# A state space scan in two passes of two channel groups, on pairs of real and imaginary part

## The chip, the cores and the metric

The kernel runs on one core of one Trainium2 chip. The metric is device time in microseconds (us) of one execution; the numbers are medians of three runs. TensorE multiplies matrices, VectorE, ScalarE and GpSimd compute elementwise, and SyncE, ScalarE and GpSimd also issue DMAs, each on a queue of its own. [...]

## What is computed

The program is two transformer blocks on 256 latent and 256 context tokens of width 1024: attention, then a state space layer (S5), then a second block. The change is in S5. Each of its 128 groups of 16 channels has 64 complex states in each of two directions; a state goes on by x(t+1) = a x(t) + B u(t). It runs over the context first and goes on over the latents; only the latents' outputs are wanted.

```python
def _s5_direction(u_ctx, u_lat, lam, dt, bmat, cmat):
    ...
    def run(u, h0):
        ...
        h_fin, ys = lax.scan(step, h0, chunks)
        return h_fin, ys.swapaxes(0, 1).reshape(bsz, n, S5_GROUPS * S5_GROUP)

    h0 = jnp.zeros((u_lat.shape[0], S5_GROUPS, S5_STATE), jnp.complex64)
    h_ctx, y_ctx = run(u_ctx, h0)
    _, y_lat = run(u_lat, h_ctx)
    return y_ctx, y_lat
```

The outputs go through gelu and two large products (`glu`, `w_out`).

## The kernel before, in words

All products are of float32 values as a high and a low part. A weight piece [128, 1024] (`weight`) arrives by a DMA on SyncE's queue, ScalarE casts its high part (L97) and VectorE subtracts the low one (L98); there are two buffers for the parts, so a cast waits until TensorE is done with the piece before the last one. Three matmuls make one product (L119 to L121).

S5 (`s5_layer`) works in blocks of 8 tokens, 32 of the context and 32 of the latents, and on four channel groups b = 0 to 3 of 32 pairs (direction, state pair) by 128 partitions. For each b there are

- four linears `u(b, j)`: 48 matmuls each. `s5_store_u` copies the result on ScalarE (two instructions, tile `s_ut`) and stores it to DRAM from ScalarE's queue; `s5_load_u` brings it back in another layout (tile `s_U`) from GpSimd's queue. It is a transposition by way of DRAM.
- `s5_blocks`: four steps a of 64 small matmuls (tile `vps`), which give what each block adds to the states. Each needs one operator of 1 MB (`d_rt`). ScalarE copies the result to `s_V`.
- `s5_scan` on VectorE: 16 steps, each of two products, a sum over both parts, and a difference and a sum over one part each (L493 to L497). Five levels of a tree over the 32 blocks of the context; then seven steps in which four runs of eight latent blocks go on side by side; then three that carry from run to run. A last pair of copies (L517) turns the second direction.
- `s5_out`: four steps of 16 matmuls on `s_U` (`within`) and 64 on the states (`across`). Each step's `across` needs one operator of 1 MB (`d_o`), each two `within` another (`d_t`). Two copies (`s_ysb`) and eight transposes (`ytps`) end it.

Between them stand eleven `gate` linears (24 matmuls each). TensorE and VectorE keep the order that the code is written in (`self.ordered`). `run(scan, us)` writes as many steps of the scan as go with that much of TensorE's time, so the numbers in the `yield`s and in `run` place each weight's L98 among the scan's instructions. The operators go through a ring of five buffers (`operator`); after the first four, GpSimd's queue issues them, in order with the loads of `s_U`. Scan b stands beside the linears of b + 1 and the outputs of b - 1.

## Time and profile before

| | us |
|---|---|
| median of three runs | 1501.27 |
| lowest and highest run | 1500.88, 1508.71 |
| span of the profiled execution, first to last instruction | 1494.4 |
| median less that span | 6.9 |
| TensorE busy in the span | 1379.3 (92%) |
| VectorE busy in the span | 1152.3 (77%) |
| S5's scans, first to last of VectorE's instructions | 673.9 to 871.2 |

The page has one execution; times within it are counted from its first instruction. It gives the span and no time of its own for that execution, so the 6.9 us stand for what lies around. The share of TensorE over the whole span hides that S5 is another stage than the rest: there the table by stretches has to be read.

### The profile page before, as it was taken

The numbers are of one execution on the slowest core, as the hardware profiler recorded it, in microseconds if no ns is written. First come the engines' busy times: TensorE is split into PE (matmuls) and PEld (weight loads), VectorE is DVE, ScalarE is ACT, GpSimd is POOL, SyncE is SP. The second block draws the span as 40 slices with busy tenths as digits, with TensorE's granted clock in tenths as the row PEclk, the third lists the DMA queues.
The fourth block names the chain that finished last, engine by engine and source line by source line (L and its number), as shares of the span: only waits on it lengthen the run. The fifth ranks groups of instructions, "written<-read, shape, count | busy, mean of one in ns | idle before, by whom it ended". The sixth has DMA issues, their size and how long they took to land.

```text
span 1494.4 us, 30436 instructions
## 1 busy us (share of the span) xinstructions
PE 1379.3 (92%) x12192; PEld 1201.1 (80%) x12192; DVE 1152.3 (77%) x2122; ACT 712.5 (48%) x1307; POOL 100.5 (7%) x221
## 2 busy tenths in 40 slices
PE   5889979999999998898877779999998999999997
PEld 4657656667777778798866669999998999999996
DVE  7989886787768779839988966755568876788887
ACT  4434435655555544622244244544447556565554
POOL 0012211110011011001111000000000000000000
PEclk9989988999999999999988989999999999999999
DMA  9459984454435444578787676555555544445552
GB/s 359 160 170 319 297 247 127 141 156 143 140 120 156 149 131 139 174 223 282 276 294 281 246 266 212 194 194 198 184 183 164 171 169 141 158 171 192 187 184 99
DMA packets 140622, 291.35 MB, mean 195 GB/s; under 512 B 30480, under 2 KB 70080, under 8 KB 135104
## 3 DMA queue, kind: packets, MB, share of 16 engines
q1 hardware_dynamic: 108592, 232.01, 45.5%
q0 software_dynamic: 11360, 49.34, 10.4%
q10 hardware_dynamic: 20528, 8.06, 2.0%
q8 instruction: 95, 1.56, 0.4%
q14 instruction: 47, 0.39, 0.1%
HBM read 234.83 MB, written 54.53 MB: 194 GB/s over the span
## 4 chain that ended last, share of the span: by engine, by line
PE 69%; DVE 15%; issue 7%; DMA 6%; ACT 2%; POOL 0%; SPq 0%; DVEq 0%; ACTq 0%; POOLq 0%
PE lin L119 14%; PE lin L120 14%; PE lin L121 13%; PE modps L591 3%; DVE s_t L493 3%; DVE wl L98 2%; DMA sp_x<-in_s_bcw_dram 2%; PE slat L119 2%; DMA d_o<-sp_o 1%; PE sctx L119 1%; PE dn L121 1%; PE dn L119 1%; PE dn L120 1%; DVE s_V L495 1%; DVE sp_t L37 1%
## 5 line engine op out<-in xcount | busy, mean ns | idle before, releaser
L97 ACT CAST wh<-wr 128x1024 fp32r<-128x1024 f32 x268 | 280.5, 1048 | 407.2 <-PE lin L120 250.0
L98 DVE TENSOR_TENSOR wl<-wr,wh 128x1024 fp32r<-128x1024 f32 x268 | 327.5, 1223 | 148.2 <-ACT wh L97 147.7
L119 PE MATMUL lin<-prH,wh 128*128 128x256 f32 x512 | 145.3, 284 | 0.0
L119 PE MATMUL lin<-yaH,wh 128*128 128x256 f32 x512 | 144.8, 283 | 0.0
L120 PE MATMUL lin<-yaL,wh 128*128 128x256 f32 x512 | 144.6, 282 | 0.0
L121 PE MATMUL lin<-prH,wl 128*128 128x256 f32 x512 | 143.7, 281 | 1.0 <-DVE wl L98 1.0
L121 PE MATMUL lin<-yaH,wl 128*128 128x256 f32 x512 | 144.1, 281 | 0.0
L120 PE MATMUL lin<-prL,wh 128*128 128x256 f32 x512 | 143.8, 281 | 0.2 <-DVE prL L109 0.2
L120 PEld LDWEIGHTS lin<-prL,wh 128*128 128x128 f32 x512 | 96.7, 189 | 1.7 <-DVE prL L109 0.6
L119 PEld LDWEIGHTS lin<-yaH,wh 128*128 128x128 f32 x512 | 97.5, 190 | 0.0
L119 PEld LDWEIGHTS lin<-prH,wh 128*128 128x128 f32 x512 | 96.7, 189 | 1.0
L121 PEld LDWEIGHTS lin<-yaH,wl 128*128 128x128 f32 x512 | 97.4, 190 | 0.0
L120 PEld LDWEIGHTS lin<-yaL,wh 128*128 128x128 f32 x512 | 97.3, 190 | 0.0
L121 PEld LDWEIGHTS lin<-prH,wl 128*128 128x128 f32 x512 | 96.3, 188 | 1.2 <-DVE wl L98 1.2
L493 DVE TENSOR_TENSOR s_t<-s_V,s_tab 128x256 f32<-128x256 f32 (+2 forms) x120 | 73.2, 652 | 15.7 <-ACT s_V L475 14.5
L121 PE MATMUL u<-h,wl 128*128 128x256 f32 x224 | 66.0, 295 | 9.3 <-DVE wl L98 9.3
L427 POOL DMA_DIRECT2D d_t<-sp_g x128 | 66.8, 529 | 56.9 <-DVE sp_g L37 52.6
L121 PE MATMUL lin<-h,wl 128*128 128x256 f32 x128 | 42.4, 331 | 29.7 <-DVE wl L98 29.7
L119 PE MATMUL u<-h,wh 128*128 128x256 f32 x224 | 66.1, 295 | 0.0
L120 PE MATMUL u<-h,wh 128*128 128x256 f32 x224 | 65.6, 293 | 0.5 <-issue 0.5
L119 PE MATMUL lin<-hH,wh 128*128 128x512 f32 x144 | 60.6, 421 | 0.7 <-ACT hH L103 0.7
L37 DVE TENSOR_TENSOR sp_t<-s_pb,sp_x 128x1024 f32<-128x1024 f32 x64 | 60.0, 952 | 0.6
(481 smaller groups left out, 3871.8 us busy)
## 6 DMA issues: line engine op xcount, KB each, us to landing
wr<-in_glu_dram SPq DMA_DIRECT2D x64, 512.0 KB, 3.3
wr<-in_w_up_dram SPq DMA_DIRECT2D x44, 512.0 KB, 4.2
wr<-in_w_in_dram SPq DMA_DIRECT2D x32, 512.0 KB, 4.8
mraw<-in_w_mod_dram SPq DMA_DIRECT2D x64, 256.0 KB, 3.1
d_rt<-sp_rt SPq DMA_DIRECT2D x64, 256.0 KB, 4.0
d_o<-sp_o SPq DMA_DIRECT2D x32, 512.0 KB, 4.8
wr<-in_s_in_dram SPq DMA_DIRECT2D x32, 512.0 KB, 4.5
s_op<-d_o POOLq DMA_DIRECT2D x16, 1024.0 KB, 7.9
```

What stands on the lines that cost most here:

```text
L37: return lambda *a, **k: self.net.in_order(f(*a, **k))
L97: self.in_order(nc.scalar.copy(hi, raw))
L98: self.in_order(nc.vector.tensor_tensor(lo, raw, hi.bitcast(F32), SUB))
L119: self.in_order(t.matmul(out, a[0], b[0], start=start, stop=False))
L120: self.in_order(t.matmul(out, a[0], b[1], start=False, stop=False))
L121: self.in_order(t.matmul(out, a[1], b[0], start=False, stop=stop))
L427: nc.gpsimd.dma_start(self.d_t[k].rearrange("s i j e c -> i s j e c")[:, :, j, e], a)
L493: go(v.tensor_tensor(t[:, x], src.to_broadcast([128, 2, 32, n]), a[x].unsqueeze(1).to_broadcast([128, 2, 32, n]), MUL))
L495: go(v.tensor_tensor(dst, dst, t[:, 0], ADD))
L591: self.in_order(nc.tensor.matmul(p[32 * j:32 * j + 32, :w], self.cs[:, kc, :], raw[:, jj * w:jj * w + w], start=(kc == 0), stop=(kc == 7), ...
```

## The change

The four channel groups are scanned two at a time, so there are two scans instead of four, with rows of 64 pairs. Real and imaginary part lie side by side. A step is two products and two sums, all over both parts; the second product reads the pairs swapped and multiplies by (-imaginary, imaginary). The context's blocks lie in a tile of their own (`s_C`) with a tree of four levels and one step into the last block; then the latents' 32 blocks go one by one in 31 steps (`s_V`, `at`). Both directions read their own block, so there is no reversal at the end. The multipliers are the powers 1, 2, 4, 8 and 16 alone.

`U` is one tile with context and latents apart, so `d_u` is written in runs of 32 floats (128 bytes) instead of 64, and each load is two DMAs. In S5 `s_ut` has one buffer instead of two, and the operators' ring four instead of five. The order is written anew: blocks 0, four linears, blocks 1; scan 0 beside six linears and blocks 2 and 3; scan 1 beside the outputs 0 and 1 and all eleven gates; then the outputs 2 and 3.

```diff
     def s5_scratch(self):
...
-        self.d_u = d.tile([4, 4, 8, 128, 64], F32, name="d_u")
+        self.d_u = d.tile([4, 4, 8, 2, 128, 32], F32, name="d_u")
...
-    def s5_store_u(self, b, j, ps, tp):
+    def s5_store_u(self, b, j, ps, tp, bufs=2):
...
-        nc.scalar.dma_start(self.d_u[b, j].rearrange("s p k -> p s k")[:, ::-1], ut.rearrange("p s g k -> p s (g k)"))
+        nc.scalar.dma_start(self.d_u[b, j].rearrange("s g p k -> p (s g) k"), ut.rearrange("p s g k -> p (s g) k"))
...
-        t = self.ops.tile([128, 2048], F32, name="s5_op", bufs=5)
+        t = self.ops.tile([128, 2048], F32, name="s5_op", bufs=4)
...
+        def step(a, src, swapped, t, base, dst):
+
+            for x, y, z in ((src, a[0], base), (swapped, a[1], dst)):
+                go(v.tensor_tensor(t, x, y.to_broadcast(t.shape), MUL))
+                go(v.tensor_tensor(dst, z, t, ADD))
+        for l in range(4):
...
+                i, o = slice(c + h - 1, e, m), slice(c + m - 1, e, m)
+                n, x = (e - c) // m, Cf[:, :, o]
+                step(a, Cf[:, :, i], Cf[:, :, i, ::-1], T[:, :, 0:n], x, x)
...
+        step(one(4), x, x[:, :, :, ::-1], Tv, base, at((0, 31)))
+        for k in range(31):
+            c, o = (k, 31 - k), at((k + 1, 30 - k))
+            step(one(0), at(c), at(c, 1), Tv, o, o)
...
     def s5_layer(self, h1):
...
-                self.s5_store_u(b, j, self.u(b, j, h1), tp)
+                self.s5_store_u(b, j, self.u(b, j, h1), tp, 1)
...
+            for a in range(4):
+                st[0][2](0, a, ahead[a])
+            for b, j in ((1, 2), (1, 3), (2, 0), (2, 1)):
+                u(b, j)
+            blocks(1)
+            scan += [self.s5_scan(0, st[0], tp), 0.0]
+            for b, j in ((2, 2), (2, 3), (3, 0), (3, 1), (3, 2), (3, 3)):
+                linear(b, j)
+            st[1] = self.s5_blocks(tp)
+            blocks(2)
+            blocks(3)
+            run(scan, 1000.0)
+            scan += [self.s5_scan(1, st[1], tp), 0.0]
...
+            for b in range(2):
+                within, across, close = out(b, st[0][1])
+                for a in range(4):
+                    within(a)
+                    across(a)
+                    run(scan, 2.3)
+                    if a % 2 == 1:
                         gate(1)
...
```

How the change stands in the engines' orders, at three places. ScalarE where S5 begins, around the first blocks' copies (`s_ut` is the copy and store of a linear, `vps` the blocks' result), before:

```order
L97 CAST wh<-wr 128x1024
L438 COPY s_ut<-u 128x8x32 x2
L439 DMA d_u<-s_ut 128x8x64
L97 CAST wh<-wr 128x1024
L438 COPY s_ut<-u 128x8x32 x2
L475 COPY s_V<-vps 128x2x256
L439 DMA d_u<-s_ut 128x8x64
L475 COPY s_V<-vps 128x2x256 x7
```

and now:

```order
L97 CAST wh<-wr 128x1024
L435 COPY s_ut<-u 128x8x32 x2
L436 DMA d_u<-s_ut 128x16x32
L97 CAST wh<-wr 128x1024
L435 COPY s_ut<-u 128x8x32 x2
L436 DMA d_u<-s_ut 128x16x32
L474 COPY s_C<-vps 128x2x128
L475 COPY s_V<-vps 128x2x4x31
```

The second copy into `s_ut` now has the same buffer as the first, and the first blocks' copies, two for each bank of `vps`, stand behind it; the store's runs went from 64 floats to 32.

VectorE at the scan's way from the context's tree into the latents (`s_t` is the product, `s_tab`, `s_a`, `s_tr` and `s_ti` are multipliers), before:

```order
L493 TENSOR_TENSOR s_t<-s_V,s_a_7182 128x64 x2
L495 TENSOR_TENSOR s_V<-s_V,s_t 128x64
L496 TENSOR_TENSOR s_V<-s_V,s_t 128x32
L497 TENSOR_TENSOR s_V<-s_V,s_t 128x32
L493 TENSOR_TENSOR s_t<-s_V,s_tab 128x64x4 x2
L495 TENSOR_TENSOR s_V<-s_V,s_t 128x64x4
L496 TENSOR_TENSOR s_V<-s_V,s_t 128x32x4
L497 TENSOR_TENSOR s_V<-s_V,s_t 128x32x4
L98 TENSOR_TENSOR wl<-wr,wh 128x1024
```

and now, at the same place of scan 0:

```order
L497 TENSOR_TENSOR s_t<-s_C,s_tr 128x64x2
L498 TENSOR_TENSOR s_V<-s_C,s_t 128x2x32x2
L497 TENSOR_TENSOR s_t<-s_C,s_ti 128x64x2
L498 TENSOR_TENSOR s_V<-s_V,s_t 128x2x32x2
L98 TENSOR_TENSOR wl<-wr,wh 128x1024
L497 TENSOR_TENSOR s_t<-s_V,s_tr 128x64x2
L498 TENSOR_TENSOR s_V<-s_V,s_t 128x2x32x2
```

Four instructions of 128 elements, each reading what the one ahead of it wrote, take the place of five; this L98 is the last one in scan 0, and 31 such steps follow it.

TensorE at the end of S5 (`yps` from `s_U` is `within`, from `s_V` it is `across`; `lin<-yaH` is the first product of `glu`), before:

```order
L536 MATMUL yps<-s_op,s_U 32x128 x8
L549 MATMUL yps<-s_op,s_V 32x128 x32
L560 MATMUL ytps<-ident,s_ysb 128x128 x8
L536 MATMUL yps<-s_op,s_U 32x128 x32
L549 MATMUL yps<-s_op,s_V 32x128 x128
L560 MATMUL ytps<-ident,s_ysb 128x128 x8
L119 MATMUL lin<-yaH,wh 128x256
```

and now:

```order
L540 MATMUL yps<-s_op,s_U 32x128 x32
L553 MATMUL yps<-s_op,s_V 32x128 x128
L564 MATMUL ytps<-ident,s_ysb 128x128 x8
L540 MATMUL yps<-s_op,s_U 32x128 x8
L553 MATMUL yps<-s_op,s_V 32x128 x32
L564 MATMUL ytps<-ident,s_ysb 128x128 x8
L119 MATMUL lin<-yaH,wh 128x256
```

Before, the four `across` of one group stand behind the last scan; now those of group 2 do, and all of group 3's output (four such pairs of `within` and `across`; one is shown).

## Rows read from the trace of the kernel before

**Rows 1.** Stretches of S5: us, PE, PEld, DVE, ACT, POOL busy, clock, DMA, GB/s

```profile
660.40:673.20 12.80, 9.95 (x259) 9.42 (x257) 9.91 (x20) 5.69 (x10) 0.00 (x0) 0.87 0.83 282
673.20:721.00 47.80, 42.54 (x523) 41.41 (x523) 46.29 (x89) 14.56 (x26) 8.96 (x16) 0.96 0.80 268
721.00:771.00 50.00, 39.92 (x750) 37.21 (x750) 43.56 (x86) 15.61 (x30) 6.75 (x12) 0.86 0.82 298
771.00:821.00 50.00, 38.51 (x735) 35.15 (x732) 43.61 (x86) 18.44 (x35) 6.74 (x12) 0.90 0.77 284
821.00:871.00 50.00, 34.65 (x508) 31.07 (x510) 47.99 (x90) 12.09 (x19) 4.11 (x7) 0.90 0.67 249
```

**Rows 2.** The same for the scans' instructions alone, four scans together (tile s_V)

```profile
673.80:871.20 197.40, 14.26 (x768) 10.78 (x768) 158.34 (x328) 13.73 (x25) 0.90 0.77 275
```

**Rows 3.** Waits: who waited for whom, us in total, times, longest

```profile
PE lin L121 <- DVE wl L98: 26.6, 10, 6.1
POOL s_U L446 <- DMA d_u<-s_ut: 65.1, 10, 19.8
DVE s_t L493 <- ACT s_V L475: 14.5, 3, 6.3
```

**Rows 4.** TensorE's price of four linears, blocks of one group, one output step

```profile
637.40:660.40 23.00, 23.00 (x193) 22.93 (x192) 4.58 (x8) 5.91 (x13) 0.72 (x2) 1.00 0.65 191
763.40:771.10 7.70, 7.70 (x258) 7.63 (x257) 2.09 (x4) 6.36 (x10) 1.79 (x3) 1.00 0.61 231
866.60:868.30 1.70, 1.70 (x81) 1.26 (x80) 1.21 (x3) 1.10 (x2) 0.54 (x1) 1.00 0.83 308
```

**Rows 5.** VectorE in time, multipliers: floats alone, in twos, in fours, 32 bytes apart

```profile
658.97 0.41 DVE L334 TENSOR_TENSOR s_tab<-s_t 128x128 f32<-128x128 f32 x1
659.41 0.41 DVE L335 TENSOR_TENSOR s_t<-s_tab 128x128 f32<-128x128 f32 x1
661.43 0.43 DVE L334 TENSOR_TENSOR s_tab<-s_t 128x256 f32<-128x256 f32 x1
664.47 0.69 DVE L334 TENSOR_TENSOR s_tab<-s_t 128x512 f32<-128x512 f32 x1
```

**Rows 6.** VectorE in time: small steps of the first scan's tree

```profile
688.74 0.39 DVE L495 TENSOR_TENSOR s_V<-s_V,s_t 128x128 f32<-128x128 f32 x1
689.16 0.27 DVE L496 TENSOR_TENSOR s_V<-s_V,s_t 128x64 f32<-128x64 f32 x1
```

**Rows 7.** VectorE's groups by line and shape, 671 to 871 us: busy, mean ns

```profile
L98 DVE TENSOR_TENSOR wl<-wr,wh 128x1024 fp32r<-128x1024 f32 x22 | 26.7, 1215 | 0.8 <-ACT wh L97 0.8
L517 DVE COPY s_V<-s_V 128x496 f32<-128x496 f32 x8 | 3.0, 412 | 0.0
```

**Rows 8.** A linear's store, all stores' landing, U's loads' landing; packets by queue

```profile
L439 ACTq DMA_DIRECT2D d_u<-s_ut x1: 366/366/366, 659.8 to 659.8; - x1
DMA to landing us min/median/max: 2.8/5.6/16.0
DMA to landing us min/median/max: 2.5/3.8/7.8
q0 software_dynamic: 278, 2.02, 69.4%
q10 hardware_dynamic: 2079, 0.52, 30.1%
```

**Rows 9.** End of S5: operator's load, its landing, TensorE, the chain's last load

```profile
867.61 0.54 POOL L451 DMA_DIRECT2D s_op<-d_o  x1 [8.51 <-PE yps L536]
DMA to landing us min/median/max: 6.1/6.1/6.1
880.26 1.96 PE L549 MATMUL yps<-s_op,s_V 64*32 64x128 f32 x64 [1.36 <-DMA s_op<-d_o]
885.06 0.56 PE L119 MATMUL lin<-yaH,wh 128*128 128x256 f32 x1
872.08 8.14 DMA s_op<-d_o
```

More of the change, by code (lines that the diff above doesn't have):

```diff
@@ L475, in step @@
[L475 to L502 removed]
+                                p[64 * e:64 * e + 64, c:c + 64], rt[:, d, j, r, 64 * e:64 * e + 64],
@@ L503, in s5_scan @@
             h, m = 1 << l, 2 << l
[L504 removed]
+            a = self.tr[:, g, l].unsqueeze(2).unsqueeze(3), self.ti[:, g, l].unsqueeze(2)
+            for c in ((0, 16) if l == 0 else (0,)):
                 e = c + 16 if l == 0 else 32
[L506 to L511 removed]
@@ L1115, in s5_layer @@
             self.ordered = (mybir.EngineType.PE, mybir.EngineType.DVE)
-            st, prev = self.s5_blocks(0, tp, ahead), None
-            for a in range(4):
-                st[2](a)
-            todo = iter([(b, j) for b in range(1, 4) for j in range(4)][2:])
+            st = [self.s5_blocks(tp), None]
+            scan = []
             ya = []
@@ L1130, in low @@
                                                           ya[0][:, j:j + 2].bitcast(F32), SUB))
-            for b, (nu, early, late) in enumerate(((5, 0, 1), (3, 0, 1), (2, 1, 1), (0, 12 - NG, 0))):
-                scan = [self.s5_scan(b, st, tp), 0.0]
-                cur = st
-                if prev:
-                    within, across, close = out(b - 1, prev)
-                if b == 3:
-                    ya.append(self.big.tile([128, 16, 256], F32R, tag="s16", name="yaH", bufs=3))
-                    high(0)
-                    high(1)
-                for a in range(max(nu, 4 if prev else 0)):
-                    if a < nu:
-                        u(*next(todo))
-                        run(scan, 4.0)
-                    for _ in range((early + 3 - a) // 4):
-                        gate(1)
-                        run(scan, 2.6)
-                    if prev and a < 4:
-                        within(a)
-                        across(a)
-                        run(scan, 2.7)
-                if prev:
-                    close()
-                if b < 3:
-                    st = self.s5_blocks(b + 1, tp)
-                    for a in range(4):
-                        if a < late:
-                            gate(1)
-                            run(scan, 1.5)
-                        st[2](a)
-                        run(scan, 2.0)
-                else:
-                    high(2)
-                    within, across, close = out(3, cur)
-                    for a in range(4):
-                        within(a)
-                run(scan, 1000.0)
-                prev = cur
@@ new lines, in s5_layer @@
+            st[1] = self.s5_blocks(tp)
[3 more added lines that the diff above has]
+            scan += [self.s5_scan(1, st[1], tp), 0.0]
+            ya.append(self.big.tile([128, 16, 256], F32R, tag="s16", name="yaH", bufs=3))
+            left = 16 - NG
+            for b in range(2):
+                within, across, close = out(b, st[0][1])
+                for a in range(4):
+                    within(a)
+                    across(a)
+                    run(scan, 2.3)
+                    if a % 2 == 1:
+                        gate(1)
+                        left -= 1
+                        run(scan, 1.6)
+                close()
+                high(b)
@@ L1169, in s5_layer @@
+            for _ in range(left):
+                gate(1)
+                run(scan, 1.6)
+            within, across, close = out(2, st[1][1])
+            for a in range(4):
+                within(a)
+            run(scan, 1000.0)
             ya.append(self.big.tile([128, 16, 256], F32R, tag="s16", name="yaL", bufs=3))
@@ L1171, in s5_layer @@
                 across(a)
-                if a < 3:
+                if a < 2:
                     low(a)
+            close()
+            high(2)
+            within, across, close = out(3, st[1][1])
+            for a in range(4):
+                within(a)
+                across(a)
+            low(2)
             close()
```

132 lines of the change are left out of this document (61 added, 71 removed).

## The prediction

> **What bounds the kernel now.** I read the table by stretches first, since the change touches S5 alone and the orders of the engines ahead of it and behind it stay as they are. From 673 to 871 us VectorE is busy 43.6 to 48.0 us of every 50 [rows 1], TensorE 34.7 to 42.5, and less from stretch to stretch. The scans hold VectorE for 158.3 of 197.4 us [rows 2], 22 weights' subtractions for 26.7 [rows 7], and 14.5 go to three hand-overs, in which the next scan waits for ScalarE's copy of its blocks [rows 3]; together 199.5, the stretch but for some overlap. So VectorE sets the pace. TensorE's waits are its consequence: 26.6 us in the gates' linears for a subtraction that stands behind scan steps [rows 3]. DMA is not far behind, busy 0.67 to 0.82 [rows 1].
>
> What TensorE must do from 660.4 us to the first product of `glu` at 885.1 [rows 9] follows from three prices [rows 4]: four linears 23.0, so 5.8 each and 2.9 for a gate of half the matmuls; the blocks of a group 7.7; an output step 1.7. Ten linears, eleven gates, four groups' blocks, 16 output steps and some 4 for transposes make 58 + 32 + 31 + 27 + 4 = 152 us, in 224.7. That difference of 73 us is the most that there is to gain.
>
> **A scan step after the change.** Multipliers lying 32 bytes apart cost 0.41 us for 128 floats and 0.43 for 256 in twos [rows 5]: a float's neighbour is free. Floats alone cost 0.27 for 64 and 0.39 for 128 [rows 6]. The new step in the latents has 64 pairs, so 0.27 to 0.28 for an instruction. One that needs the one ahead of it starts 0.03 after its end (688.74 and 0.39, next at 689.16) [rows 6], and one that only overwrites what that one reads does as well (658.97 and 0.41, next at 659.41) [rows 5]. All four instructions hang together in this way: 4 x 0.305 = 1.22 us. In the tree a step of 1024 floats takes 4 x 1.25 = 5.0 (1.22 for 1024 [rows 7]), three times; 512 floats 4 x 0.72 = 2.9; 256 floats 4 x 0.46 = 1.8. With the step into the last block and 31 in the latents a scan is 15 + 2.9 + 1.8 + 32 x 1.22 = 58.7 us, two are 117.4, against 158.3 busy now. The hand-overs of 14.5 go as well, since the second scan's blocks are ready when it begins. The multipliers themselves (20 small instructions for 24) lie ahead of the first blocks' end and cost nothing either way.
>
> **What the change puts in series.** The saving of 55 us on VectorE is not the gain, because three stretches now have no scan beside them or wait for something else. I follow the path on the clock of before, from 660.4.
>
> 1. Ahead of scan 0. TensorE does blocks 0 (12.8 with their waits [rows 1]), four linears (23.2) and blocks 1 (7.7), and ScalarE copies the last bank (0.8): 704.9 at the earliest, where the first scan now starts at 673.8 [rows 2]. But the four linears (1,0) to (1,3) go through one buffer `s_ut`: each copy (0.65 for two) waits until the store before it has landed, and blocks 1 need the last one. Stores take 2.8 to 16.0 us to land, median 5.6 [rows 8], the long ones while operators load. Their runs are half as long and twice as many. The first of the four is stored at 659.8 now [rows 8]; I set it 2 us later, since the stores ahead of it have the short runs too. At 5 each the chain is hidden; at 14 it is 661.8 + 4 x 14.65 = 720.4. I take 9, because two of the four meet four operators in flight: 661.8 + 4 x 9.65 = 700.4, then the loads of `U` (two issues of 0.54 [rows 9], 3.8 to land [rows 8]) 705.3, blocks 1 713.0, copy 713.8. ScalarE's casts and the copies of blocks 0 stand behind the waiting copies; this delays blocks 0 by some 4 us, which is inside the same chain. Scan 0 starts at **714** (705 to 734).
>    Whether 9 or 14 is right hangs on how engines share their time: in a stretch with two operators and two stores in flight, 2079 store packets passed beside 278 of the operators, 7.5 to one [rows 8]. If a queue gives a fixed number of packets per turn, twice the packets take twice the turns; if a turn is one partition's packets (8 now, 16 then), the turns stay as many. [...] No run here shows which.
> 2. Scan 0. 58.7 and five subtractions at 1.13, and 0.6 for casts that come late: 65 us, to **779**. TensorE has six linears and two groups' blocks beside it, 50 us, with some 10 of waiting for operators: hidden, then idle until 779.
> 3. Scan 1. 58.7 and 13 subtractions, 73.4. Here the cover turns: a subtraction waits for its cast, the cast for the gate two before it, and the first four gates stand between the output steps of groups 0 and 1, which need 12 operators of 1 MB through a ring of four. Two loads behind the first of three took 6.5 us (first landed at 867.6 + 6.1, last at 872.08 + 8.14 [rows 9]), so 3.3 each and some 40 in all, of which four are in or under way when scan 1 begins. By this the fourth gate is done 36 us into scan 1, where VectorE asks for what depends on it at 33; its cast then makes VectorE wait some 5 us, and the cast for the seventh, which stands behind the sixth gate's silu on ScalarE, as much again. I take 10 (0 to 20). Scan 1 ends at **862**, where the last now ends at 871.2.
> 4. The tail. Now one group's `across` is left, three loads late, and `glu` starts 13.9 us after the scan (885.1 - 871.2). After the change the ring holds group 2's four operators when scan 1 ends, so all six of group 3 load from then on: 1.1 for the first `across`, 6.1 to the first landing, five more at 3.0 (less traffic beside them than the 3.3 above; bounds 2.7 and 3.5), 1.1 for the last `across` and 2.9 from there to `glu` (880.26 + 1.96, then 885.06 [rows 9]): 26.1 us. `glu` starts at **888**.
>
> That is 3 us after the 885.1 of now. The profiled span of 1494.4 becomes 1497.4; the runs' median lies 6.9 above the span, and I carry that over: 1501.3 + 3 = **1504 us**. So the saving on VectorE is spent on 40 us that pass before the first scan, on the waits in scan 1 and on a tail that is 12 us longer.
>
> **Rivals.**
>
> - *The buffers don't bind* (faster). The stores land in about 5, so scan 0 starts at 705; the gates keep ahead of VectorE, no wait in scan 1; the tail's loads come at 2.7. 705 + 65 + 73.4 + 24.6 = 868: 17 us gained, **1484**. For it speaks that half of the stores land within 5.6 us [rows 8]; against it the maximum of 16.0 there, and 65.1 us in which GpSimd waited for such stores [rows 3]. Half of it gives 1492. Chance of over 0.5% faster: 0.25.
> - *Twice the packets take twice the turns* (slower). With a fixed number of packets per turn a store beside operators lands in 14 instead of 9, scan 0 starts at 734, and the time is **1524**; from 11 each it is past 0.5%. For it speaks the 7.5 to one [rows 8], which is near the 8 runs that a partition has now; that same number speaks against it, if the turn goes by partitions. Chance 0.14.
> - *The swapped operand is slow* (slower). Read in falling order, a pair may cost as two single floats, 0.39 instead of 0.28 for 64 pairs and about twice for the tree: 64 x 0.12 + 2 x (3 x 0.9 + 0.7) = 14 us, **1518**; it decides from 0.06 a small instruction. Against it: the copies of 496 floats in falling order take 0.41 [rows 7], faster than any product of that size. Chance 0.10.
> - Scan 1 and the tail both at their upper ends (20 and 28.5): +16, **1517**. Chance 0.08.
>
> **How the numbers follow.** A measurement of this kernel tells about 0.5%, 7.5 us, from no change. The forecast, within it (1494 to 1509), has 0.43; the faster rival 0.25; the three slower ones 0.32. The predicted time is the forecast's, 1504. The range of 8 in 10 reaches to 1487 (nearly the whole of the faster rival) and to 1521 (the slow operand and the tail in it, the packets' end out); the forecast's own range is 1494 to 1509.
>
> **What would show it.** VectorE's small products at 0.28 and a step's pitch of 1.22 show the price; the swapped product beside the plain one shows the third rival. The first product on `s_C` at 714 and a row of ScalarE waiting for d_u<-s_ut show step 1; at 705 without that row, the first rival. A scan 1 of 83 us with VectorE waiting for ScalarE's casts shows step 3, of 74 not. In the tail the `yps` matmuls should wait for s_op loads, 26 us from the last scan instruction to `lin<-yaH`. I am wrong if `glu` starts ahead of 877 or after 893.

## The result and the profile after

The changed kernel takes **1524.2 us** (median of 4 runs, 1523.5 to 1525.4) where the kernel before takes 1501.1: a ratio of 1.0153, with a 95% interval of 1.0125 to 1.0180. The forecast was 1504, with a range of 1487 to 1521. So it is slower, by 23 us, and lies 3 us beyond the upper end of the range.

The executions wander by 5 to 9 us ahead of the layer, where the programs are the same. I therefore measure from a mark, the first product of the linear (0,2), which lies at 637.34 us in the profile of before and at 642.45 in that of the changed kernel (636 to 645 in the other runs). `glu` starts 247.7 us behind the mark before the change (885.06 [rows 9]) and 269.6 behind it after. Before, 36.5 of these pass until the first scan starts, 197.4 in the scans and 13.9 behind them; after, 83.8, 159.9 and 25.9. So the scans give back 37.5 us, and the stretches ahead of them and behind them take 59.3 more. These are the rows of TensorE in time in the changed kernel (start, duration, engine, line, operation; in brackets the idle time ahead and what ended it):

```profile
642.45 0.28 PE L119 MATMUL u<-h,wh 128*128 128x256 f32 x1
666.51 0.34 PE L469 MATMUL vps<-s_U,s_op 128*64 128x64 f32 x4 [0.86 <-DMA s_U<-d_u]
...
886.22 6.34 PE L553 MATMUL yps<-s_op,s_V 64*32 64x128 f32 x256 [22.26 <-DVE s_V L498]
...
898.08 1.81 PE L553 MATMUL yps<-s_op,s_V 64*32 64x128 f32 x64 [2.69 <-DMA s_op<-d_o]
...
905.53 1.96 PE L553 MATMUL yps<-s_op,s_V 64*32 64x128 f32 x64 [1.66 <-DMA s_op<-d_o]
...
912.05 0.36 PE L119 MATMUL lin<-yaH,wh 128*128 128x256 f32 x1
```

The stretches of the layer after the change, cut at the scans (us, busy time of PE, PEld, DVE, ACT, POOL, granted clock, DMA share, GB/s), which answer to [rows 1, 2]:

```profile
673.00:700.00 27.00, 25.41 (x372) 25.03 (x370) 2.45 (x2) 8.02 (x20) 3.44 (x6) 0.94 0.86 308
700.00:726.00 26.00, 17.43 (x315) 16.89 (x314) 1.23 (x1) 9.04 (x23) 6.36 (x11) 0.80 0.67 173
726.00:793.00 67.00, 53.34 (x816) 51.59 (x815) 61.88 (x153) 21.13 (x52) 12.60 (x22) 0.95 0.81 263
793.00:886.00 93.00, 58.16 (x968) 52.75 (x968) 70.81 (x162) 28.43 (x50) 8.22 (x14) 0.79 0.66 248
886.00:912.00 26.00, 18.42 (x591) 14.79 (x592) 3.87 (x7) 6.68 (x16) 3.57 (x6) 0.76 0.67 251
```

VectorE, busy through 673 to 871 before, now does next to nothing for 53 us (2.45 and 1.23 busy), works through scan 0, idles a quarter of scan 1 and has nothing to do in the tail. Its groups by line and shape from 726 to 886 us (busy, mean ns, idle time before and who ended it), which answer to [rows 6, 7]:

```profile
L498 DVE TENSOR_TENSOR s_V<-s_V,s_t 128x128 f32<-128x128 f32 x126 | 37.0, 294 | 4.3
L98 DVE TENSOR_TENSOR wl<-wr,wh 128x1024 fp32r<-128x1024 f32 x18 | 22.0, 1221 | 17.5 <-ACT wh L97 17.3 <-issue 0.2
L497 DVE TENSOR_TENSOR s_t<-s_V,s_ti 128x128 f32<-128x128 f32 x62 | 18.2, 293 | 2.1
L497 DVE TENSOR_TENSOR s_t<-s_V,s_tr 128x128 f32<-128x128 f32 x62 | 18.1, 292 | 1.8
L498 DVE TENSOR_TENSOR s_C<-s_C,s_t 128x1024 f32<-128x1024 f32 x12 | 14.7, 1228 | 0.4
```

The scan itself is as cheap as it was meant to be: 0.293 us for a small instruction, and the product that reads pairs in falling order (with `s_ti`) costs what the plain one costs. Scan 0 takes 66.9 us; without its five subtractions at 1.13 that is 61.2 for a scan, 122 for two (113 of them busy), against 158 busy and 14.5 of hand-overs before. What was lost lies around it. The waits of the layer from 660 to 930 us (total, times, longest), which answer to [rows 3]:

```profile
POOL s_U L444 <- DMA d_u<-s_ut: 74.9, 11, 15.2
DVE wl L98 <- ACT wh L97: 71.0, 10, 20.6
...
ACT s_ut L435 <- DMA d_u<-s_ut: 20.4, 6, 9.9
...
DVE s_t L497 <- ACT s_C L474: 16.7, 1, 16.7
...
PE yps L553 <- DMA s_op<-d_o: 6.0, 3, 2.7
```

VectorE's 71.0 for casts are 53.7 ahead of scan 0 and behind scan 1, and 17.3 in scan 1 (the 17.3 in the groups above).

### The profile page after: what moved, and what is told of

Read it like the earlier page. It is cut to its first block, busy times and chain, and to the rows that moved or that the text cites. A ratio compares the mean times of both kernels' runs of the same rounds, so it can differ in the third digit from the quotient of the medians.

```text
span 1523.5 us, 30488 instructions
## 1 busy us (share of the span) xinstructions
PE 1383.5 (91%) x12192; PEld 1204.8 (79%) x12192; DVE 1102.3 (72%) x2086; ACT 716.7 (47%) x1343; POOL 108.8 (7%) x233
## 4 chain that ended last, share of the span: by engine, by line
PE 69%; DVE 12%; DMA 10%; issue 7%; ACT 2%; POOL 0%; SPq 0%; DVEq 0%; ACTq 0%; POOLq 0%
PE lin L119 14%; PE lin L120 14%; PE lin L121 13%; PE modps L595 3%; DVE s_t L497 2%; DMA d_u<-s_ut 2%; PE slat L119 2%; DVE wl L98 2%; DMA sp_x<-in_s_bcw_dram 1%; DMA mraw<-in_w_mod_dram 1%; PE sctx L119 1%; PE dn L121 1%; PE dn L119 1%; DMA d_o<-sp_o 1%; PE dn L120 1%
## 5 line engine op out<-in xcount | busy, mean ns | idle before, releaser
L98 DVE TENSOR_TENSOR wl<-wr,wh 128x1024 fp32r<-128x1024 f32 x268 | 327.7, 1224 | 208.8 <-ACT wh L97 197.3
L97 ACT CAST wh<-wr 128x1024 fp32r<-128x1024 f32 x268 | 280.4, 1048 | 388.5 <-PE lin L120 255.7
L120 PEld LDWEIGHTS lin<-prL,wh 128*128 128x128 f32 x512 | 96.7, 189 | 1.7 <-DVE prL L109 0.6
L424 POOL DMA_DIRECT2D d_t<-sp_g x128 | 66.8, 529 | 59.9 <-DVE sp_g L37 55.6
L119 PE MATMUL u<-h,wh 128*128 128x256 f32 x224 | 63.6, 284 | 0.0
L120 PE MATMUL u<-h,wh 128*128 128x256 f32 x224 | 63.4, 283 | 0.0
L37 DVE TENSOR_TENSOR sp_t<-s_pw,sp_x 128x1024 f32<-128x1024 f32 x64 | 59.7, 953 | 0.8
L120 PE MATMUL lin<-hL,wh 128*128 128x512 f32 x144 | 58.7, 408 | 0.7 <-DVE hL L104 0.7
```

The costliest lines, as they stand in the source:

```text
L37: return lambda *a, **k: self.net.in_order(f(*a, **k))
L97: self.in_order(nc.scalar.copy(hi, raw))
L98: self.in_order(nc.vector.tensor_tensor(lo, raw, hi.bitcast(F32), SUB))
L119: self.in_order(t.matmul(out, a[0], b[0], start=start, stop=False))
L120: self.in_order(t.matmul(out, a[0], b[1], start=False, stop=False))
L424: nc.gpsimd.dma_start(self.d_t[k].rearrange("s i j e c -> i s j e c")[:, :, j, e], a)
```

## The experiments

All times of stretches are read from each kernel's own trace; "start" and "glu" count from the mark, "waits" are VectorE's for casts inside scan 1. Each row's stretches are those of one execution. The changed kernel's two differ by 0.3 us at the start, by 1.4 in scan 1, by 1.6 in its waits and in the tail, and by 2.7 at `glu`; differences of that size between rows say nothing.

| kernel | start of scan 0 | scan 0 | scan 1 | waits | tail | glu | time over before (95%) |
|---|---|---|---|---|---|---|---|
| before | | | | | 13.9 | 247.7 | 1 |
| changed | 83.8 | 66.9 | 93.0 | 17.3 | 25.9 | 269.6 | 1.0153 (1.0125 to 1.0180) |
| changed, again | 83.5 | 66.8 | 94.4 | 18.9 | 27.5 | 272.3 | 1.0164 (1.0136 to 1.0192) |
| two store buffers | 75.5 | 66.8 | 91.8 | 16.2 | 27.5 | 261.7 | 1.0094 (1.0067 to 1.0120) |
| runs of 256 bytes | 79.3 | 66.8 | 91.7 | 16.1 | 26.8 | 264.7 | 1.0103 (1.0060 to 1.0146) |
| the same, again | 80.1 | 66.7 | 92.6 | 16.9 | 25.7 | 265.2 | 1.0140 (1.0114 to 1.0166) |
| half operators | 73.7 | 66.8 | 88.3 | 12.4 | 24.3 | 253.2 | 1.0018 (0.9999 to 1.0037) |
| scan 1 without its steps | 82.0 | 66.9 | 24.2 | | 74.3 | 247.4 | 1.0026 (1.0008 to 1.0044) |
| gates ahead | 81.9 | 69.6 | 85.8 | 14.8 | 26.4 | 265.5 | 1.0128 (1.0102 to 1.0154) |
| paced | 82.9 | 66.8 | 84.6 | 9.2 | 30.2 | 264.6 | 1.0132 (1.0101 to 1.0162) |
| prefetched tail | 83.7 | 66.7 | 95.5 | 19.9 | 16.2 | 262.2 | 1.0115 (1.0089 to 1.0142) |
| combined | 74.4 | 69.6 | 91.0 | 19.8 | 16.9 | 252.0 | 1.0040 (1.0023 to 1.0056) |
| combined, paced | 80.4 | 69.6 | 72.4 | 2.4 | 29.2 | 251.8 | 1.0012 (0.9992 to 1.0032) |
| rearranged | 79.5 | 74.1 | 73.3 | 3.2 | 20.5 | 247.5 | 0.9991 (0.9969 to 1.0013) |
| linears ahead | 70.0 | 74.1 | 73.3 | 3.3 | 18.9 | 236.4 | 0.9941 (0.9920 to 0.9962) |

### Is VectorE still the bound? Scan 1 without its steps

```diff
-        for k in range(31):
+        for k in range(0 if g else 31):
```

> The changed kernel with the 31 steps through the latents left out of the second scan (its output is not the reference's): 40.6 us less on VectorE. If VectorE sets the end of scan 1: all of it comes back, the first product of glu at 872 instead of 912, 1484. If operators and gates on TensorE end nearly as late (it ends its last gate at 862 and the inner products of group 2 at 864): only some 22 us come back, glu at 890, 1502, which is what the kernel before takes.

Measured: 40.6 us less on VectorE bring 22 back (glu at 247.4 instead of 269.6; 1503.2 us). This is the expected number of the second reading: about half of scan 1's steps cost nothing, since TensorE gets through gates and output steps hardly sooner: its last gate ends 215.8 us behind the mark, and 219.6 in the changed kernel. Its two longest groups of waits from the start of scan 1 to `glu`:

```profile
PE yps L553 <- DMA s_op<-d_o: 10.9, 5, 2.9
PE yps L553 <- DVE s_V L498: 6.8, 1, 6.8
```

Even with a second scan that costs next to nothing, the order of the changed kernel is not faster than the kernel before.

### The late first scan: buffer, operators, length of the runs

The chain of work that ended last (start, duration, what) runs through the stores of group 1:

```profile
664.58 5.54 DMA d_u<-s_ut
670.51 9.77 DMA s_op<-d_rt
691.00 15.04 DMA d_u<-s_ut
706.79 4.00 DMA d_u<-s_ut
711.89 4.15 DMA s_U<-d_u
716.17 9.64 PE vps L469 x244
```

GpSimd in time shows the store between them, issued at 670.88, and which operators the slow ones met:

```profile
675.52 0.58 POOL L449 DMA_DIRECT2D s_op<-d_rt  x1 [3.43 <-PE vps L469]
688.57 1.19 POOL L444 DMA_DIRECT2D s_U<-d_u  x2 [12.46 <-DMA d_u<-s_ut]
689.74 1.69 POOL L449 DMA_DIRECT2D s_op<-d_rt  x3
706.57 1.24 POOL L444 DMA_DIRECT2D s_U<-d_u  x2 [15.15 <-DMA d_u<-s_ut]
```

The four stores take 5.5, 17.7 (from its issue to GpSimd's next load), 15.0 and 4.0 us: the two slow ones stand beside operators that were asked for just ahead of or behind them. Three kernels tell the causes apart. **A second buffer** (the memory that the output steps use later, so that no other memory is given up):

```diff
-        ut = tp.tile([128, 8, 2, 32], F32, name="s5_ut", bufs=bufs)
+        if bufs == 1 and j % 2:
+            ut = tp.tile([128, 8, 4, 2, 16], F32, name="s5_ysb", bufs=1).rearrange("p t a e s -> p (t a e s)")
+            ut = ut[:, 0:512].rearrange("p (s g k) -> p s g k", s=8, g=2)
+        else:
+            ut = tp.tile([128, 8, 2, 32], F32, name="s5_ut", bufs=bufs)
```

> The changed kernel with a second buffer for the stores of the linears (every other one goes through the memory that the output steps use later); nothing else moves. If the single buffer makes the chain ahead of the first scan: the copies no longer wait for the store just before, the last of the four stores leaves when its linear ends (about 695) instead of 706.8, and with 10 us to land, 5 for the loads and 9 for the blocks the first scan starts at 718 to 720 instead of 726.3; 1517 us. If the landing of the stores beside operators sets it: two stores share the time that one had, the first scan stays at 725 or later, 1524.

Measured: the first scan starts 8.3 us earlier, 1515.0 us. (1,1) now leaves 2 us behind (1,0), ahead of the operators, and has landed by 674.6, when GpSimd loads it back. The three operators that stood behind that load in GpSimd's queue, and were asked for together from 689.74 on, are now asked for one by one from 676 to 682, and (1,2) and (1,3) land in 5.6 and 4.7 us. The buffer's price is where it puts the stores.

**The operators at half the size:**

```diff
-        t = self.ops.tile([128, 2048], F32, name="s5_op", bufs=4)
-        (q or self.nc.gpsimd).dma_start(t if len(src.shape) == 2 else t.rearrange("p (k c) -> p k c", k=2), src)
+        t = self.ops.tile([128, 1024], F32, name="s5_op", bufs=4)
+        (q or self.nc.gpsimd).dma_start(t, src[:, 0:1024] if len(src.shape) == 2 else src[:, 0])
...
-                                p[64 * e:64 * e + 64, c:c + 64], rt[:, d, j, r, 64 * e:64 * e + 64],
+                                p[64 * e:64 * e + 64, c:c + 64], rt[:, 0, j, r, 64 * e:64 * e + 64],
...
-                        ts[-1][:, a % 2, j, e],
+                        ts[-1][:, 0, j, e],
...
-                                p[e][32 * j:32 * j + 32, a * 128:a * 128 + 128], st, O[es, d, r, j],
+                                p[e][32 * j:32 * j + 32, a * 128:a * 128 + 128], st, O[es, 0, r, j],
```

> The changed kernel with operators of half the size: each load of S5's operators brings 0.5 MB instead of 1, and the products use that half twice (the output is not the reference's). The number of loads, the ring of four and every order stay. If the traffic of the operators makes the late stores, the waits in scan 1 and the tail: first scan at 715 instead of 726, scan 1 in 76 us instead of 93, the tail in 16 instead of 26, 1486 in all. If the waits in scan 1 come from the order of gates and casts: scan 1 stays at 90 or more, 1503.

Measured: the first scan starts 10.1 us earlier, as expected; but scan 1 keeps 12.4 of its 17.3 us of waits, and the tail is shorter by 1.6 and not by 10. So the traffic makes the late start, and it makes neither the greater part of the waits in scan 1 nor the length of the tail. The whole gain was 20 us in the runs' ratio, half of it at the start.

**The runs at their old length:**

```diff
-        nc.scalar.dma_start(self.d_u[b, j].rearrange("s g p k -> p (s g) k"), ut.rearrange("p s g k -> p (s g) k"))
+        nc.scalar.dma_start(self.d_u[b, j].rearrange("s g (p x) k -> (g p) s (x k)", x=2), ut.rearrange("p s g k -> p s (g k)"))
```

> The changed kernel with its stores in 1024 runs of 64 floats instead of 2048 of 32; the loads keep their form, so U holds the same bytes in another order and the output is not the reference's. If a queue's turn is one partition's packets: the two stores that meet operators (17.7 and 15.0 us to land) stay within 2 us, the first scan starts at 724 to 728, 1524. If it is a number of packets: they land in about 9 and 8, the first scan starts at 711 to 713, 1510.

The first time its runs were 8 us faster than the changed kernel and its profile 5, so both ran once more on one chip:

> The changed kernel itself, as the standard beside the next one on the same chip: 1.0153 of the kernel before again, within 0.3%; the first scan 82 to 85 us behind the linear (0,2)'s first product, its two stores beside operators 14 to 18 us to land, scan 1 in 92 to 94, the tail in 26.

> The changed kernel with stores in 1024 runs of 64 floats once more (the output is not the reference's), beside the changed kernel on the same chip. If the length of the runs has a part in the late first scan: 4 to 8 us less than the changed kernel, with the stores beside operators 3 to 4 us shorter on the mean. If the 8 us between them came from the chip and the day: within 2 us of it.

GpSimd in time, the changed kernel first:

```profile
690.36 1.19 POOL L444 DMA_DIRECT2D s_U<-d_u  x2 [12.88 <-DMA d_u<-s_ut]
691.53 1.68 POOL L449 DMA_DIRECT2D s_op<-d_rt  x3
707.55 1.24 POOL L444 DMA_DIRECT2D s_U<-d_u  x2 [14.34 <-DMA d_u<-s_ut]
```

and with long runs:

```profile
687.48 1.19 POOL L444 DMA_DIRECT2D s_U<-d_u  x2 [12.12 <-DMA d_u<-s_ut]
688.65 1.68 POOL L449 DMA_DIRECT2D s_op<-d_rt  x3
703.04 1.25 POOL L444 DMA_DIRECT2D s_U<-d_u  x2 [12.71 <-DMA d_u<-s_ut]
```

The stores (1,1), issued at 672.95 and 670.36, are waited for until 690.36 and 687.48: 17.4 and 17.1 us, the same. The stores (1,2), issued at 691.94 and 692.28, until 707.1 and 702.6 (the next store's copy starts there): 15.1 and 10.3. So one of the two slow stores does not feel the length of the runs, the other gets a third shorter. The first scan starts 3.4 us earlier in this pair and 4.5 in the first. The time differs by 1.7 us in the medians (1521.3 and 1519.6), with overlapping intervals, so it doesn't tell the two apart. At the start, five executions with short runs and the same program up to there show 82.0 to 83.8 us, the two with long runs 79.3 and 80.1: some 3 us are clear of that spread. Why the two stores differ isn't settled.

The same buffer taken from the kernel **before**:

```diff
-        ut = tp.tile([128, 8, 2, 32], F32, name="s5_ut", bufs=2)
+        ut = tp.tile([128, 8, 2, 32], F32, name="s5_ut", bufs=1 if b else 2)
```

> The kernel before with one buffer instead of two for the stores of the twelve linears inside the layer. If a single buffer costs by the place of the store (behind operators) and not by the form of the scan: the linears (1,1) to (1,3) are late here too, but the first scan needs group 0 alone and starts as before at 13 us behind the first block; the second scan waits up to 8 us more; 1501 to 1508. If it costs nothing here: 1499.

Measured: 1504.6 us, 1.0029 of the kernel before (1.0013 to 1.0044). The first scan starts 2.2 us later behind the mark, the hand-overs grow from 14.5 to 17.6. There a scan stands beside most of the linears, which I take to be why so little of the late stores shows; after the change none does.

Two other parts of the change, the operators' ring of four instead of five and the loads of `U` as two DMAs each, have no run of their own.

### The waits in scan 1

In the changed kernel they stand ahead of 825.40 (1.8 us), 833.55 (5.7), 844.14 (6.9), 851.38 (2.3) and 864.12 (0.7). For the longest, ScalarE in time shows what the cast (L97) stood behind:

```profile
832.47 1.05 ACT L97 CAST wh<-wr 128x1024 fp32r<-128x1024 f32 x1 [1.88 <-PE lin L120]
833.42 0.38 ACT L952 ACTIVATE s_sg<-lin 128x256 f32<-128x256 f32 x1
833.82 1.28 ACT L1097 ACT_TABLE_LOAD   x1
...
835.11 2.15 ACT L1097 ACTIVATE y<-ytps 128x128 f32<-128x128 f32 x8
837.28 1.28 ACT L952 ACT_TABLE_LOAD   x1
...
842.79 0.38 ACT L952 ACTIVATE s_sg<-lin 128x256 f32<-128x256 f32 x1 [2.81 <-DMA d_sg<-s_sg]
843.07 1.04 ACT L97 CAST wh<-wr 128x1024 fp32r<-128x1024 f32 x1
```

A gate's silu, the eight gelus of the group that ended there, a table load of 1.28 us for each of the two changes between the functions, and a silu that waited 2.8 us for the store of an earlier gate: 9.6 us in ScalarE's queue between two casts. No operator is waited for in it, but the store may be late beside operators in flight: with operators of half the size that silu doesn't wait for a store, and VectorE waits 4.0 us here instead of 6.9.

TensorE waits for an operator once in scan 1, for 1.7 us; the other two of its three such waits above (2.7 and 1.7) are in the tail:

```profile
828.33 1.16 PE L553 MATMUL yps<-s_op,s_V 64*32 64x128 f32 x64 [1.69 <-DMA s_op<-d_o]
```

The products of an output step take 1.8 us (0.64 for `within`, 1.16 here). Even so eight steps, four gates and the transposes took 40.3 (793.2 to 833.4). The first two gates took 6.7 and 8.5 us, the third and fourth 3.1: the first two wait for their subtractions (1.8 and 3.0), which stand behind steps of the tree, and part of their products ran at a lower clock (granted 0.75 and 0.65 over these two gates, 1.00 over the next two). So VectorE's order had 6.2 us of steps (2.3 twice and 1.6) for two output steps and a gate, in which TensorE took 10.

Two kernels move the order and leave the loads. **Four gates ahead of the blocks of group 1:**

```diff
-            for b, j in ((1, 2), (1, 3), (2, 0), (2, 1)):
+            for b, j in ((1, 2), (1, 3)):
                 u(b, j)
+            gate(4)
             blocks(1)
...
-            for b, j in ((2, 2), (2, 3), (3, 0), (3, 1), (3, 2), (3, 3)):
+            for b, j in ((2, 0), (2, 1), (2, 2), (2, 3), (3, 0), (3, 1), (3, 2), (3, 3)):
...
-            left = 16 - NG
+            left = 7
```

> The changed kernel with four of its eleven gates between the linears (1,3) and the blocks of group 1, in the place of the linears (2,0) and (2,1), which go beside the first scan; so seven gates are left beside the second scan. If the waits in scan 1 (17 us over its 61 of steps and 15 of subtractions) come from the hand to hand order of subtraction, gate and cast: the first scan starts at the same time and takes 2 us more, the second has 5 us of subtractions less and about half of the waits, 80 us instead of 93; 1513. If they come from operators that arrive late through the ring of four: as many operators in the same time, the waits stay, scan 1 takes 88 and the kernel 1521.

Measured: scan 1 in 85.8, between the two expectations; four subtractions less are 4.5, the waits only fall from 17.3 to 14.8. The number of gates is not what makes them. **The place of the subtractions in VectorE's order:**

```diff
-                    run(scan, 2.3)
+                    run(scan, 4.6)
```

> The changed kernel with one number changed in the order of VectorE: beside each output step of groups 0 and 1 stand scan steps worth 4.6 us instead of 2.3, so that the gates' subtractions stand two steps later for each output step that precedes them; gates, loads and all other orders stay. In the changed kernel an output step with its operators took TensorE about 5 us, and VectorE came to the subtraction before its cast could run. If this place in the order makes the waits of scan 1 (17 us): most of them go, scan 1 takes 80 us instead of 93, 1513. If late operators make them wherever the subtractions stand: the last gate ends at 862 as before, the steps behind the last subtraction are few, and the waits are only moved; scan 1 stays at 88 to 93, 1521 or more.

Measured: scan 1 in 84.6, with waits of 9.2: about half of them are made by the place in the order, and 8.4 us come back there, of which 4.3 are lost again in the tail (30.2). (The 5 us that the expectation gives an output step "with its operators" are the 40.3 divided by eight; they are mostly the gates between the steps.) TensorE now waits for the later subtractions, from 794 to 909 us:

```profile
PE lin L121 <- DVE wl L98: 17.7, 5, 6.4
PE yps L553 <- DVE s_V L498: 8.6, 2, 5.7
```

(5.2 and 29.6 in the changed kernel over the same part.) The gates end at 873.9 instead of 862, the inner products of group 2 behind them hold two places of the ring until then, and the operators of the tail come later. By their times neither kernel can be told from the changed one (1.0128 and 1.0132 beside 1.0153 and 1.0164, intervals overlapping); what they show is in the stretches.

### The tail

```diff
...
+            pre = []
+            for name, k in (("s5_C", 1), ("s5_V", 2)):
+                t = tp.tile([128, 2, 2, 16, 32, 2], F32, name=name, bufs=k).rearrange("p d b q k r -> p (d b q k r)")
+                for x in (t[:, 0:2048], t[:, 2048:4096]):
+                    nc.gpsimd.dma_start(x, self.d_o[12 + len(pre)])
+                    pre.append(x)
+            within3, across3, close3 = out(3, st[1][1], "ps", pre)
+            for a in range(4):
+                within3(a)
             run(scan, 1000.0)
...
-            within, across, close = out(3, st[1][1])
             for a in range(4):
-                within(a)
-                across(a)
+                across3(a)
...
```

> The changed kernel with all loads of group 3 ahead of the end of scan 1: its two operators of the inner products go through the ring behind those of group 2, its four of the outer products into the memory of s_C (free after the tree) and of the first s_V (free after group 1's output). If the tail of 26 us is six loads in a row through the ring: what is left is TensorE's 64 x 4 x 2 products with their transposes, 18 us; 4 MB more stand beside the gates' weights and cost scan 1 up to 2 us; 1517. If the tail is TensorE's and ScalarE's own chain (half operators left it at 24.3): 25 us and 1524.

Measured: a tail of 16.2 us, TensorE's own work with two copies of ScalarE between:

```profile
888.86 5.46 PE L553 MATMUL yps<-s_op,s_V 64*32 64x128 f32 x248 [20.82 <-DVE s_V L498]
...
896.33 1.09 PE L564 MATMUL ytps<-ident,s_ysb 128*128 128x128 f32 x8 [1.18 <-ACT s_ysb L560]
897.36 2.04 PE L553 MATMUL yps<-s_C,s_V 64*32 64x128 f32 x128
...
904.14 1.09 PE L564 MATMUL ytps<-ident,s_ysb 128*128 128x128 f32 x8 [1.21 <-ACT s_ysb L560]
```

Of the 9.7 us, 4.9 are TensorE's waits for operators (2.69, 0.53 and another 1.66 in the changed kernel's tail), 3.7 are group 3's `within`, which now run ahead of the scan's end, and the rest is that the eight `across` took 11.9 us instead of 13.3. The waits are those of a ring: a product frees a place, GpSimd issues, and 5.2 to 10.0 us pass until the operator has landed. The six loads go in two turns, four from 888.6 on and two from 900.2 on, and the last lands 21.7 us behind the scan. With half the bytes it lands after 17.9, so most of this is the turn and not the transfer, and TensorE still waits 3.8. Scan 1 is 2.5 us longer with the extra loads, 1.1 beside the changed kernel's second profile.

### Together, and a version that is faster than both

Second buffer, four gates ahead and the prefetched tail together:

> Second store buffer, four gates ahead and the prefetched tail together. If the three terms are separate: 9 + 11 + 7 = 27 us less than the changed kernel, 1497, as fast as the kernel before or faster by up to 5 us. If they lean on one another (the gates take the place that the earlier start freed, the prefetched loads delay the gates' weights): 1508.

Measured: 1505.0 us; glu 17.6 us earlier, where the three terms alone give 7.9, 4.1 and 7.4: 19.4. They nearly add up. Scan 1 keeps 19.8 us of waits, so with the steps at the measured pace (4.6 for an output step, 2.8 for a gate) in the same kernel:

> Second store buffer, four gates ahead, prefetched tail, and the scan steps placed by the measured pace (4.6 us for an output step, 2.8 for a gate). Without it scan 1 took 91 us there, 20 of them waits. If the place in the order makes them: scan 1 in 74 to 78, glu 13 to 17 us earlier, 1490, faster than the kernel before by about 0.6%. If the operators make them: 1502 to 1505.

Measured: 1501.0 us. In its profile, the slowest of its twelve executions, the first scan starts 6 us later than in the one without pacing, where nothing ahead of it differs; so much does the start wander between executions with two buffers. The waits are gone (2.4), scan 1 takes the 72.4 that its instructions need, and the tail grows to 29.2: `within` of group 3 stood ahead of `across` of group 2 in the ring and held two places until the late gates were done. The wait moved on to the next thing in line. With those operators in other memory and the inner products ahead of the last gates:

```diff
-            us = [self.u(1, j, h1) for j in range(2)]
+            us = [self.u(1, j, h1) for j in range(3)]
...
-            for b, j in ((1, 2), (1, 3), (2, 0), (2, 1)):
-                u(b, j)
+            u(1, 3)
+            gate(3)
             blocks(1)
...
+            for _ in range(2):
+                gate(1)
+                run(scan, 2.0)
...
-                    run(scan, 2.3)
+                    run(scan, 3.8)
...
-            for _ in range(left):
-                gate(1)
-                run(scan, 1.6)
             within, across, close = out(2, st[1][1])
             for a in range(4):
                 within(a)
+            for _ in range(left):
+                gate(1)
+                run(scan, 2.4)
```

> The changed kernel's scan (the same instructions) in another order around it: second store buffer; the linear (1,2) ahead of group 0's blocks, where TensorE waited for loads; three gates ahead of group 1's blocks, two beside the first scan, six beside the second with 3.8 and 2.4 us of steps for an output step and a gate; group 2's inner products ahead of the last two gates; both of group 3's inner operators and two of its outer ones loaded ahead of the end of scan 1 into s_C and the first s_V. If the loss of 23 us lies in what stands around the scan and not in the scan: first scan 66 to 72 us behind the linear (0,2)'s first product (84 in the changed kernel), 61 us and 10 subtractions for it, 61 and 8 for the second with at most 5 us of waits, a tail of 17: glu 225 to 235 behind that product (248 in the kernel before, 270 in the changed one), 1480 to 1490. If the waits come back in another place (gates late, operators late at the end): 1500.

Measured: 1497.3 us, level with the kernel before. The waits and the tail are as expected; the first scan is not (79.5 instead of 66 to 72): the one store left behind the blocks of group 0, (1,3), met three operators and took 15.4 us; (1,2), issued just behind two operators, took 18.3. So that linear goes ahead too, and all four now stand ahead of the loads of group 0:

```diff
+            us = [self.u(1, j, h1) for j in range(4)]
             for j in range(4):
                 self.s5_load_u(0, j, tp, nc.sync)
-            us = [self.u(1, j, h1) for j in range(3)]
...
-            for j in range(3):
+            for j in range(4):
...
-            u(1, 3)
             gate(3)
             blocks(1)
```

> The rearranged kernel with the linear (1,3) ahead of group 0's blocks as well, so that all four stores of group 1 leave before the operators of group 1's blocks are asked for. In the rearranged kernel that one store met three operators, took 15.4 us to land and held TensorE for 12.2. If such meetings make the late first scan: no store of group 1 takes over 10 us, the blocks of group 1 follow the three gates without a wait, the first scan starts 58 to 64 us behind the linear (0,2)'s first product (79.5 in the rearranged kernel), and the kernel takes 1480 to 1486, 1% less than the kernel before. If the operators themselves are late instead: the first scan at 72, 1491.

Measured: **1488.2 us**, 0.9941 of the kernel before (0.9920 to 0.9962), with the same scan; `glu` starts 33 us earlier than in the changed kernel. The first scan starts at 70.0, later than the 58 to 64 expected: a store, (1,2), still took 15.5 us beside the operators of group 0. The stretches of this kernel, from the mark to `glu`:

```profile
636.20:670.90 34.70, 34.70 (x292) 34.57 (x290) 9.48 (x24) 8.53 (x22) 4.71 (x9) 1.00 0.81 220
670.90:706.20 35.30, 27.28 (x589) 26.65 (x589) 4.90 (x4) 16.07 (x42) 6.34 (x12) 0.90 0.99 330
706.20:780.40 74.20, 69.48 (x959) 67.68 (x957) 66.39 (x157) 26.71 (x62) 14.60 (x25) 1.00 0.83 253
780.40:853.70 73.30, 44.78 (x912) 38.76 (x912) 65.17 (x157) 22.04 (x40) 10.64 (x18) 0.81 0.88 350
853.70:872.60 18.90, 12.69 (x528) 11.57 (x529) 3.73 (x7) 6.76 (x16) 1.06 (x2) 0.85 0.37 124
```

Ahead of scan 0 the DMA engines are now busy 0.99 of the time, which may be what bounds that part; no run tests it. In scan 0 TensorE is busy 69.5 of 74.2, in scan 1 VectorE waits 3.3 us for casts.

## Why the prediction was wrong, by its steps

| step | forecast | measured | difference |
|---|---|---|---|
| 1, start of scan 0 behind the mark (714 - 637.3) | 76.7 | 83.8 | +7.2 |
| 2, scan 0 | 65 | 66.9 | +1.9 |
| 3, scan 1 | 83.4 | 93.0 | +9.6 |
| 4, tail | 26.1 | 25.9 | -0.2 |

Together 18.5 us. The forecast's 3 above the kernel before and these give 21.5 of the 23.1 measured; the profile shows another 2.1 us between the start of `glu` and the end (611.5 instead of 609.3). That the profiled execution of before was some 5 us quicker than its median was carried over rightly: median less span was 6.9 there and is 0.7 here, and the mark moved by 5.1.

**The price of a step** held in kind and was 7% short: 0.293 us instead of 0.28, a pitch of 1.31 instead of 1.22, which is 2.8 us in each scan. The neighbour of a float is not quite free: 64 pairs take 0.293 where 64 floats alone took 0.27 [rows 6]. The swapped operand's rival is refuted by the two groups with `s_ti` and `s_tr`, 293 and 292 ns.

**Step 1** had the right chain: one buffer, four landings, with two of them beside operators. It failed in the size. 9 us a landing were put in; 5.5, 17.7, 15.0 and 4.0 are 10.6 on the mean, or 6.2 us in all, since the two beside operators took 15 and 17.7 and not the 13 that a mean of 9 stands for. The chain began 3.0 us earlier than put (its first copy is 21.5 behind the mark, put at 24.5), the copy of (1,2) waited 1.8 behind a cast on ScalarE, and the blocks of group 1 took 9.6 for 7.7: in these 9.6 us TensorE waited for no operator, and its granted clock was 0.52 over the first 4.8 of them and 1.00 over the rest (1.00 over the 7.7 [rows 4]). No run shows how the engines divide their time between the queues, on which the choice of 9 over 14 hung. The rival of the packets, in which twice the packets take twice the time, is a part of it: the length of the runs made 3 to 4 us, on one store of two. That 1524 was also this rival's time is a coincidence: it put 20 us on the first scan alone.

**Step 3** is the step that failed most: it put 10 us of waits, and they were 17.3; the price of the steps makes the rest of its 9.6. Two of the waits stood where it had them. VectorE waited 5.7 us for the cast behind the fourth gate (forecast some 5) and 6.9 for the seventh's, which stood behind the sixth gate's silu (forecast as much again). The other three, 4.7 us together, were not in the sum. The cause given for the late fourth gate was wrong: it was done 39.3 us into the scan (forecast 36), but not because 12 operators took 40 us through the ring of four, for TensorE waited for one of them once, 1.7 us. It was late because the first two gates waited for subtractions behind tree steps (1.8 and 3.0 us) and ran in part at a lower clock (0.75 and 0.65 over the two). With half the operators' bytes 12.4 us of waits remained; 2.9 of the 4.9 that went are in the wait of 6.9, where a silu no longer waits for a store. VectorE's order, by which it came to the subtractions ahead of their casts, is the larger part: pacing alone took 8 of the 17.3 away, pacing with gates moved ahead all but 2.4 to 3.3.

**Step 4** was right in its number: the last operator lands 21.7 us behind the scan, and the sum has 22.2 up to there (1.1, 6.1 and five at 3.0). Its reason was half right. I priced the loads by their bytes, one behind the other; they come in two turns of the ring, and half the bytes bring the last landing to 17.9 only. TensorE's own products, which the sum counts at its two ends alone, are busy for 18.4 of the 25.9, and with the loads moved ahead 16.2 remain. That the sum met the 25.9 to 0.2 us is in part luck.

**The range** failed, as I read it, because steps 1 and 3 were treated as independent. Each stayed within its own bounds (705 to 734, which is 67.7 to 96.7 behind the mark, and 0 to 20 of waits), and the sum fell out of the range. They share causes: both go through ScalarE's queue, and both got shorter with operators of half the size (by 10.1 and 4.9 us). The fourth rival joined the upper ends of step 3 and of the tail; none joined step 1 with step 3.

**That the saving on VectorE is not the gain** was the main claim, and the kernel without the steps of scan 1 shows it: 40.6 us less work, 22 us less time.

## What to carry to other kernels

When a change makes the busiest engine's work shorter, cost first what then stands in series ahead of it and behind it: here scans that take 36 us less of VectorE made the kernel 23 us slower, and the same scans with the stores ahead of the large loads, the cheap work moved into the gaps and the steps placed by measured paces made it 33 us faster again. A single staging buffer cost, here, by the place in the DMA queues to which it moved a store: with a second one the first scan started 8.3 us earlier. In a chain over three engines that hand over to one another, move the waiting instruction by the pace that the trace shows, and look next at what stands behind the last link, since the wait goes there.

## What the runs showed of the hardware

In one place a store's landing beside large loads did not depend on the number of its runs: 2048 of 128 bytes and 1024 of 256 took 17.4 and 17.1 us. In another it did: 15.1 and 10.3. The first pair is what the prediction put down to turns of one partition's runs (16 or 8 of them); the second lies nearer to its turns of a fixed number of packets. No run shows that there are such turns, or why the two stores differ.

TensorE's granted clock was 0.95 in scan 0, where the engine was busy 53 of 67 us, and 0.79 and 0.76 in scan 1 and the tail. From 862.0 to 886.2, where it was busy for 2 of 24 us, it was 0.62, and for the next 5 us, through which it worked without a pause, 0.50. The 64 products of an output step took 1.96 us at 0.50 (905.53 above) and 1.16 at 1.00 (828.33). Over the layer little of the loss shows in TensorE's busy time: from the mark to `glu` the same products keep it busy for 198.0 us at a granted clock of 0.86, and for 197.3 at 0.91 before the change. In the last version it is 188.9, at 0.81 to 1.00 in the stretches above, so a part of what that one gains may be the clock's.
